# A diffusion-backbone layer: the mixer's output stage in written order, the output projection by pairs of tiles, and the sums of the down weights sooner

## The chip, the cores and the metric

The kernel runs on one core of one Trainium2 chip. A core has TensorE (PE, matrix products into PSUM), VectorE (DVE), ScalarE (ACT), GpSimd (POOL) and SyncE (SP); SP's queue issues all DMA transfers of this kernel, and 16 DMA engines carry them out. The metric is the device time of one execution in microseconds (us). The time before is 2552.67 us, median of three runs (2550.52 to 2553.85).

## The reference, cut to what matters

One layer with a short gated convolution and a bidirectional mLSTM side by side, then a gated feed-forward part with a convolution in it. 128 context tokens and 2048 latent tokens pass through the same weights, 1024 channels, four mLSTM heads of 128.

```
h   = rmsnorm(x) * (1 + scale1) + shift1
z   = h @ w_in                       # sc_b, sc_c, sc_x, q, k, v, o, gates
y_sc = sc_b * conv3(sc_c * sc_x)
h_m  = rmsnorm_heads(mlstm_bidir(q, k, v, gates)) * mh_norm * sigmoid(o)
x   = x + gate1 * (concat(y_sc, h_m) @ w_out)
h2  = rmsnorm(x) * (1 + scale2) + shift2
a, g = split(conv3(h2 @ w_up))
x   = x + gate2 * ((silu(g) * a) @ w_down)
y   = rmsnorm(x) * final_norm
```

The mLSTM is computed in chunks of 128 tokens. For a chunk the output is (scores * weights) @ v plus (query * weight) @ state for both directions, divided by a denominator, and the two directions are added.

## The kernel before, in words

All activations lie channels first. The 2176 tokens are six blocks of 384 (the last 256): BA is blocks 0 to 2, BB blocks 3 to 5. A block has two or three chunks; there are 17. Every large product is done with operands split into a rounded high part and a remainder (wh and wl for weights, hH and hL for activations): `gemm` (L201) is 8 k of three products, 24 matmuls, and `load_w` (L108) brings one weight tile of 128 output channels from DRAM (wst, two buffers), rounds it on ACT (L112) and makes the remainder on POOL in two halves (L115); wh and wl have four buffers.

The first part (to L596) computes modulation and norms, then, for BB, `vg` (v and gates), `heads` for k and q (each writes one head of a block to DRAM), `shortconv`, and the sigmoid of o. Generators of side work run between the gemms: `first_stats`, `mod_dve` (32 modulation columns on VectorE), and, in a generator of its own, `down_sums` (L554), which reads w_down, forms the sums that the last stage's seven-product scheme needs and writes them to DRAM (wsD). In the kernel before, the down sums run beside the gate projections of BB and the v projection of BA (L590 to L596). The block's activations for BA are made between them (`make_h`), in the buffers (three) that BB leaves. All this lies in a pool "start", whose memory the gate phase uses next.

`gate_phase` (L646) turns the gates into per-token weights, with k heads of BA as filler. Then `weave` (L890) runs `Sums` over the chunks from last to first (states of the backward direction, written to sD), and then `Mix` over 34 units, a unit being one chunk and two of the four heads. In each turn `weave` calls the stages of neighbouring units and then takes one or two steps of a filler: q heads, o heads, `shortconv` of BA, then 32 of the 48 steps of `out_proj`. In a Mix unit, `rows` loads R (512 KB, rows broadcast to all partitions, four buffers), `pre` adds the mask on POOL (L823) and takes the exponential on ACT (L827), `first` multiplies keys with queries (L834), weighs the queries (L837, into qs) and the scores (L838), `second` computes the output (L849, L851), the forward state (L855), denominators (L859 to L861) and the normed heads (L866 to L873), `third` transposes (L879) and gates with o (L881), `last` stores to yD (L886).

`out_proj` (L431) runs over three pairs of blocks. For each pair it goes through the eight output tiles m, and for each m through both blocks: a gemm with y, the gated residual (L462), the store to xD (L464), and the sum of squares (L466 to L470). `load_y` loads and splits the y of a block once all its chunks are done (L426 to L429). After Mix, `sums` (L226) builds operands of the up projection from xD and the norms, with the rest of `out_proj` between, and the up stage follows (L1045 to L1060), then the down stage (L1199).

What sets the order: the code is traced in the order of the program, and a planner then orders the instructions of each engine by the order of the program, by when its cost model has their operands and buffers ready, and by free buffers. Each engine, and SP's queue, then takes its instructions strictly in that order. An edge without a semaphore between two instructions of one engine fixes their order; `pin` (L106) does that for the loads and the additions in `down_sums`.

Of the kernel before, what the change touches and what calls it, by code (L numbers as in the profile page):

```python
# [18 lines left out]
P = 128  # L19
D = 1024  # L20
KT = 8
# [36 lines left out]
def hymba_kernel(ctx: ExitStack, tc: tile.TileContext, I, O):  # L58
# [49 lines left out]
    def load_w(src, n=1024):  # L108
        st = wp.tile([P, WN], F32, name="wst", bufs=2)
        Q.dma_start(st[:, :n], src)  # L110
        wh = wp.tile([P, WN], F32R, name="wh")
        S.activation(wh[:, :n], st[:, :n], AF.Copy)  # L112
        wl = wp.tile([P, WN], F32R, name="wl")
        for a in (0, n // 2):
            G.tensor_sub(wl[:, a:a + n // 2], st[:, a:a + n // 2], wh[:, a:a + n // 2].bitcast(F32))  # L115
        return wh, wl
# [200 lines left out]
    with ExitStack() as ph1:  # L317
# [66 lines left out]
        def shortconv(blocks, hs, then=None):  # L384
            for m in range(4):
                wc, wx, wb = (load_w(I["w_in"][o + m]) for o in (4, 8, 0))
                for b in blocks:
# [3 lines left out]
                    S.activation(cr[:, :n], acc[:, :n], AF.Copy)  # L391
                    yield
# [4 lines left out]
                    for s0, s1, v in spans(t0, t0 + n):  # L397
# [6 lines left out]
                                               yy[:, :, :w - 1], op0=ALU.mult, op1=ALU.add)  # L404
                    yield
# [3 lines left out]
                    if then and m == 3 and b != 1:  # L409
                        then(b // 2)  # L410
# [8 lines left out]
        def load_y(b):  # L419

            assert done >= set(chunks(b))
            t0, n = BL[b]
            yH, yL = early[b] = h_pair()
            for kh in range(2):
                yt = xp.tile([P, 4, 384], F32, name="xt")
                Q.dma_start(yt[:, :, :n], yD[4 * kh:4 * kh + 4, :, t0:t0 + n].rearrange("k p t -> p k t"))  # L426
                for k in range(4):
                    S.activation(yH[:, 4 * kh + k, :n], yt[:, k, :n], AF.Copy)
                    V.tensor_sub(yL[:, 4 * kh + k, :n], yt[:, k, :n], yH[:, 4 * kh + k, :n].bitcast(F32))  # L429

        def out_proj(grps, defer):  # L431


            def load_r(grp, m):
                xs_ = []
                for b in grp:
# [3 lines left out]
                    xs_.append(xr)  # L440
                return xs_

            seq = [(g, m) for g in range(len(grps)) for m in range(KT)]
            ws = [load_w(I["w_out"][m]) for _, m in seq[:2]]
            nx = load_r(grps[0], 0)
            for i, (g, m) in enumerate(seq):
                grp = grps[g]
                if m == 0:
                    sss = [ssp.tile([P, 384], F32, name="ss") for _ in grp]
                w, xs_ = ws.pop(0), nx  # L450
                if i + 1 < len(seq):
                    nx = load_r(grps[seq[i + 1][0]], seq[i + 1][1])
                if i + 2 < len(seq):
                    ws.append(load_w(I["w_out"][seq[i + 2][1]]))
                if g + 1 < len(grps) and m == (4, 7)[min(g, 1)]:
                    load_y(grps[g + 1][0])
                for b, ss, xr in zip(grp, sss, xs_):
                    t0, n = BL[b]
                    acc = gemm(w, early[b], n)
                    for a, e, v in spans(t0, t0 + n):  # L460
                        a, e = a - t0, e - t0
                        V.scalar_tensor_tensor(xr[:, a:e], acc[:, a:e], modT[:, 16 + m, v:v + 1], xr[:, a:e],  # L462
                                               op0=ALU.mult, op1=ALU.add)
                    Q.dma_start(xD[m][:, t0:t0 + n], xr[:, :n])  # L464
                    if m == 0:
                        S.activation(ss[:, :n], xr[:, :n], AF.Square)  # L466
                    else:
                        sq = sqp.tile([P, 384], F32, name="sq")
                        S.activation(sq[:, :n], xr[:, :n], AF.Square)
                        V.tensor_add(ss[:, :n], ss[:, :n], sq[:, :n])  # L470
                    if m == KT - 1 and b == grp[1 - g] and g + 1 < len(grps):
                        load_y(grps[g + 1][1])
                    yield
                if m == KT - 1:
                    if g == len(grps) - 1:
                        defer.append(lambda: stats(grp, sss))
                    else:
                        stats(grp, sss)
# [3 lines left out]
        with tc.tile_pool(name="start", bufs=1, side="right") as stp:  # L482
# [104 lines left out]
            side = chain(first_stats(), mod_dve())  # L587
# [5 lines left out]
            run(shortconv(BB, hs), side)  # L593
            run(side)
            go = heads(BB, hs, 20, oD, AF.Sigmoid, 1.0, by_block=True)
            dsums = down_sums()  # L596
            for b in BA:
                run(islice(go, 4), dsums)
                hs[b] = make_h(b, I["x"], 0)
            run(vg(BA, hs, load_vg(0) + load_vg(1)), dsums)  # L600
            run(dsums)
# [148 lines left out]
        class Sums:  # L750
# [42 lines left out]
            def nothing(self):  # L793
                pass

            rows = pre = third = last = nothing

        class Mix:
# [21 lines left out]
            def pre(self):  # L820
                c, hp, R = self.c, self.hp, self.R
                W = R[:, :, 0]
                G.tensor_add(W, W, bc(maskN[:, None], [P, 2, 2, P]))  # L823
                acol = colsel(self.cols, AC, max(c, 0), hp)
# [4 lines left out]
            def first(self):  # L829
                c, R = self.c, self.R  # L830
                W = R[:, :, 0]
                psS = pm.tile([P, 512], F32, name="S")
                for h in range(2):
                    PE.matmul(psS[:, h * P:(h + 1) * P], self.k2[:, h], self.q2[:, h], start=True, stop=True)  # L834
                if c >= 0:
                    self.qs = mb.tile([P, 2, 2, P], F32, name="qs", bufs=2)
                    V.tensor_tensor(self.qs, R[:, :, 1], bc(self.q2[:, :, None, :], [P, 2, 2, P]), op=ALU.mult)  # L837
                V.tensor_tensor(W, bc(psS[:, :256].rearrange("p (h t) -> p h t", h=2)[:, :, None, :],  # L838
                                      [P, 2, 2, P]), W, op=ALU.mult)

            def second(self):
                c, hp, sf = self.c, self.hp, sfs[self.hp]
                self.o2 = load2(mb, "o2", oD, c + 1, hp, 5)
                y = pm.tile([P, 2, 512], F32, name="y", bufs=2)
                for h in range(2):
                    for d in range(2):
                        o = y[:, h, d * 129:(d + 1) * 129]
                        if c >= 0:
                            PE.matmul(o, self.qs[:, h, d], sf[:, h] if d == 0 else self.sb[:, h, 1],  # L849
                                      start=True, stop=False)  # L850
                        PE.matmul(o, self.R[:, h, 0, d], self.v2[:, h], start=c < 0, stop=True)  # L851
                if 0 <= c < NL - 1:
# [4 lines left out]
                yv = y[:, :, :258].rearrange("p h (d n) -> p h d n", d=2)  # L857
                den = mb.tile([P, 2, 2], F32, name="den", bufs=2)
                V.tensor_tensor(den, yv[:, :, :, 128], colsel(self.cols, EM, max(c, 0), hp), op=ALU.max)  # L859
                V.scalar_tensor_tensor(den, yv[:, :, :, 128], -1.0, den, op0=ALU.mult, op1=ALU.max)  # L860
                V.reciprocal(den, den)  # L861
                hv = self.hv = mb.tile([P, 2, P], F32, name="hv", bufs=3)
                ss = mb.tile([P, 2], F32, name="hss", bufs=2)
                sj = mb.tile([P, P], F32, name="sj", bufs=2)
                for h in range(2):
                    S.activation(hv[:, h], yv[:, h, 0, :P], AF.Copy, scale=den[:, h, 0:1])  # L866
                    V.scalar_tensor_tensor(hv[:, h], yv[:, h, 1, :P], den[:, h, 1:2], hv[:, h],
                                           op0=ALU.mult, op1=ALU.add)
                    S.activation(sj, hv[:, h], AF.Square, accum_out=ss[:, h:h + 1])
                V.tensor_scalar(ss, ss, 1.0 / P, EPS, op0=ALU.mult, op1=ALU.add)  # L870
                G.tensor_tensor(ss, ss, mhalf[:, :2], op=ALU.pow)
                for h in range(2):
                    S.activation(hv[:, h], hv[:, h], AF.Copy, scale=ss[:, h:h + 1])  # L873

            def third(self):
                c, hp, o2 = self.c, self.hp, self.o2
                psT = pst.tile([P, 512], F32, name="st")
                for h in range(2):
                    PE.transpose(psT[:, h * P:(h + 1) * P], self.hv[:, h], ident)  # L879
                for h in range(2):  # L880
                    V.scalar_tensor_tensor(o2[:, h], psT[:, h * P:(h + 1) * P], mhn[:, 2 * hp + h:2 * hp + h + 1], o2[:, h],  # L881
# [8 lines left out]
        def weave(units, fill, extra):  # L890

            n = len(units)
            for i in range(-2, n + 4):
                for k, stage in ((-1, "second"), (0, "first"), (-3, "third"), (-4, "last"), (1, "pre"), (1, "load"), (2, "rows")):
                    if 0 <= i + k < n:
                        getattr(units[i + k], stage)()
                if not -1 <= i < n + 3:
                    continue
                next(fill, None)
                if extra and i % extra == 0:  # L900
                    next(fill, None)


# [404 lines left out]
```

## Time and profile before

| | |
|---|---|
| median of three runs | 2552.67 us |
| the profiled execution | 2555.34 us, span 2553.5 us |
| TensorE busy | 2470.7 us, 97% |
| VectorE, ScalarE, GpSimd busy | 1649.2, 1112.7, 566.4 us |
| mean granted TensorE clock | 0.985 |
| DMA | 444.60 MB, mean 174 GB/s |

In the page's groups, an instruction's time includes its way through the pipeline, so a group's sum can be more than its engine's busy time; busy times by stretches are those of the engine, with overlaps counted once. "PEclk" is the TensorE clock granted, as a share of the full one. Waits are given as the waiting instruction, what released it, and total, number and longest in us. A DMA share is the mean busy share of the 16 DMA engines.

### The profile page before, as it was taken

How to read it: one execution, taken by the hardware profiler on the slowest of the kernel's cores; microseconds unless marked ns; L12 is line 12 of the kernel's file. 1: busy time of each engine (PE TensorE's matmuls, PEld its weight loads, DVE VectorE, ACT ScalarE, POOL GpSimd, SP SyncE). 2: the span in 40 equal slices, each digit the busy share in tenths (PEclk: the TensorE clock that was granted, in tenths of full speed). 3: DMA queues.
4: the chain of work that ended last, by engine and by line, in shares of the span. 5: the costliest groups of instructions: out<-in, count | busy, mean ns of one | idle time of the engine just before them, and what ended most of it. 6: DMA issues, size and time to landing. Idle time of an engine off the chain costs nothing.

```text
span 2553.5 us, 42533 instructions
## 1 busy us (share of the span) xinstructions
PE 2470.7 (97%) x16127; PEld 2366.4 (93%) x16127; DVE 1649.2 (65%) x2741; ACT 1112.7 (44%) x2035; POOL 566.4 (22%) x470
## 2 busy tenths in 40 slices
PE   8999998999999889899999999899999999999998
PEld 8999997999999889899999999788888899999998
DVE  3993255222356666678678666877776796687586
ACT  4522142222245554455455444555554554444342
POOL 2442142211233443422112111122122100000000
PEclk9999998999999999999999999999999999999999
DMA  7771188356567887775125222522222277767674
GB/s 280 252 270 69 66 278 284 117 168 178 180 191 241 253 261 226 251 270 173 67 81 181 83 83 82 171 92 99 83 91 93 72 227 227 242 214 225 187 218 135
DMA packets 281423, 444.60 MB, mean 174 GB/s; under 512 B 23282, under 2 KB 206722, under 8 KB 279554
## 3 DMA queue, kind: packets, MB, share of 16 engines
q1 hardware_dynamic: 281218, 441.88, 53.0%
q8 instruction: 127, 2.08, 0.3%
q14 instruction: 78, 0.64, 0.1%
HBM read 335.31 MB, written 106.48 MB: 173 GB/s over the span
## 4 chain that ended last, share of the span: by engine, by line
PE 77%; DMA 8%; DVE 7%; issue 3%; ACT 3%; POOL 2%; SPq 1%; DVEq 0%; ACTq 0%; POOLq 0%
PE acc L206 8%; PE acc L208 8%; PE acc L207 8%; PE pa L1045 7%; PE pa L1047 7%; PE pa L1046 6%; PE d L1200 5%; PE d L1201 5%; PE d L1199 5%; PE pb L1045 3%; PE pb L1046 3%; PE pb L1047 3%; PE pc L1045 2%; PE pc L1046 2%; PE pc L1047 2%
## 5 line engine op out<-in xcount | busy, mean ns | idle before, releaser
L206 PE MATMUL acc<-hH,wh 128*128 128x384 f32 (+1 forms) x1536 | 515.4, 336 | 8.2 <-DVE row L462 5.5
L208 PE MATMUL acc<-hH,wl 128*128 128x384 f32 (+1 forms) x1536 | 508.0, 331 | 0.5 <-POOL wl L115 0.5
L207 PE MATMUL acc<-hL,wh 128*128 128x384 f32 (+1 forms) x1536 | 507.8, 331 | 0.0
L1199 PE MATMUL d<-bh,wh 128*128 128x272 f32 x1232 | 355.7, 289 | 0.7 <-ACT raw L1057 0.7
L1201 PE MATMUL d<-bh,wl 128*128 128x272 f32 x1232 | 356.1, 289 | 0.0
L1200 PE MATMUL d<-bl,wh 128*128 128x272 f32 x1232 | 355.4, 289 | 0.0
L1045 PE MATMUL pa<-tH,wh 128*128 128x288 f32 (+1 forms) x1056 | 347.7, 329 | 3.7 <-DVE raw L1059 2.0
L1047 PE MATMUL pa<-tH,wl 128*128 128x288 f32 (+1 forms) x1056 | 346.9, 329 | 1.0 <-DVE wl L296 1.0
L1046 PE MATMUL pa<-tL,wh 128*128 128x288 f32 (+1 forms) x1056 | 346.9, 329 | 0.0
L296 POOL TENSOR_TENSOR wl<-st,wh 128x512 fp32r<-128x512 f32 x132 | 184.2, 1396 | 696.2 <-ACT wh L295 668.4
L115 POOL TENSOR_TENSOR wl<-wst,wh 128x512 fp32r<-128x512 f32 (+1 forms) x160 | 235.2, 1491 | 441.8 <-ACT wh L112 417.5
L206 PEld LDWEIGHTS acc<-hH,wh 128*128 128x128 f32 x1536 | 292.9, 191 | 10.2 <-DVE row L462 5.1
L208 PEld LDWEIGHTS acc<-hH,wl 128*128 128x128 f32 x1536 | 292.6, 190 | 1.2 <-POOL wl L115 1.0
L207 PEld LDWEIGHTS acc<-hL,wh 128*128 128x128 f32 x1536 | 293.1, 191 | 0.3 <-issue 0.2
L988 DVE SCALAR_TENSOR_TENSOR tt<-raw,fw,tt 128x127 f32<-128x127 f32 (+4 forms) x264 | 246.1, 953 | 2.7 <-ACT tt L994 1.5
L1199 PEld LDWEIGHTS d<-bh,wh 128*128 128x128 f32 x1232 | 231.9, 188 | 1.3 <-ACT raw L1057 1.1
L1200 PEld LDWEIGHTS d<-bl,wh 128*128 128x128 f32 x1232 | 231.9, 188 | 0.2
L1201 PEld LDWEIGHTS d<-bh,wl 128*128 128x128 f32 x1232 | 231.8, 188 | 0.0
L1045 PEld LDWEIGHTS pa<-tH,wh 128*128 128x128 f32 x1056 | 198.4, 188 | 20.2 <-ACT c L1052 2.2
L1047 PEld LDWEIGHTS pa<-tH,wl 128*128 128x128 f32 x1056 | 199.1, 189 | 17.0 <-DVE wl L296 1.4
L1046 PEld LDWEIGHTS pa<-tL,wh 128*128 128x128 f32 x1056 | 198.7, 188 | 15.7
L295 ACT ACTIVATE wh<-s 128x512 fp32r<-128x512 f32 x176 | 110.9, 630 | 177.7 <-PE pc L1046 92.0
(239 smaller groups left out, 4848.6 us busy)
## 6 DMA issues: line engine op xcount, KB each, us to landing
st<-in_w_up SPq DMA_DIRECT2D x88, 512.0 KB, 4.3
us<-uD SPq DMA_DIRECT2D x48, 544.0 KB, 5.0
wst<-in_w_in SPq DMA_DIRECT2D x48, 512.0 KB, 4.0
uD<-tt SPq DMA_DIRECT2D x44, 544.0 KB, 2.7
R<-nD SPq DMA_DIRECT2D x34, 512.0 KB, 4.2
wm<-in_w_modr SPq DMA_DIRECT2D x32, 512.0 KB, 5.2
wst<-in_w_out SPq DMA_DIRECT2D x24, 512.0 KB, 4.7
st<-wsD SPq DMA_DIRECT2D x32, 384.0 KB, 3.3
```

Of the source, the lines that this page charges most:

```text
L115: G.tensor_sub(wl[:, a:a + n // 2], st[:, a:a + n // 2], wh[:, a:a + n // 2].bitcast(F32))
L206: PE.matmul(acc[:, :n], w_h, hH[:, k, :n], start=(k == 0), stop=False)
L207: PE.matmul(acc[:, :n], w_h, hL[:, k, :n], start=False, stop=False)
L208: PE.matmul(acc[:, :n], w_l, hH[:, k, :n], start=False, stop=(k == KT - 1))
L296: (G if on_pool else V).tensor_sub(wl, a, wh.bitcast(F32))
L988: V.scalar_tensor_tensor(o, i, w, o, op0=ALU.mult, op1=ALU.add)
L1045: PE.matmul(acc, wh[:, w], rh, start=(kk == 0 and i in (0, 1, 5)), stop=False, skip_group_check=True)
L1046: PE.matmul(acc, wh[:, w], rl, start=False, stop=False, skip_group_check=True)
L1047: PE.matmul(acc, wl[:, w], rh, start=False, stop=(kk == 3), skip_group_check=True)
L1199: PE.matmul(acc, wh[:, c], uh, start=(kk == 0), stop=False)
L1200: PE.matmul(acc, wh[:, c], ul, start=False, stop=False)
L1201: PE.matmul(acc, wl[:, c], uh, start=False, stop=(kk == KH - 1))
```

## The change

Three things change; the arithmetic stays.

In Mix the five methods become fifteen small stages, and `weave` gets two lists: stages called before the filler and stages called after it. The edges added by `in_order` fix, for every instruction from the first to the last of the Mix weave, the order of the program on its engine, SP's queue and the filler included. The product of queries and weights is made in place in R, so the tile qs goes.

`out_proj` goes by pairs of tiles: m and m+1 for one block, then for the other. A weight is loaded four steps ahead and split two steps later; the store and the squares of a step come at the start of the next one; the statistics of a pair of blocks come after the next pair's first gemm; y is loaded and split in steps. `shortconv` loads and splits the next tile's weights at given points, and ends with the first two weights of `out_proj`.

`down_sums` is chained behind `mod_dve` in the side work of BB, and what is left of it is run before the start pool closes; the v projection of BA comes after that pool.

```diff
+    def in_order(first):
+        behind = {}
+        for i in nc.cur_bb.bb.instructions[first:]:
+            if i.engine in behind:
+                tc.add_manual_dep(i, behind[i.engine].name, mybir.DependencyInfo(
+                    mybir.DependencyClass.NoSync, mybir.DependencyReason.DATA), reason="in_order")
+            behind[i.engine] = i
...
-        def shortconv(blocks, hs, then=None):
+        def shortconv(blocks, hs, then=None, more=(), ws=None):
+            todo = chain((I["w_in"][o + m] for m in range(4) for o in (4, 8, 0)), more)
+            ws = [] if ws is None else ws
+            ws += [load_w(next(todo)) for _ in range(3)]
...
+        def next_y(grp, ready):
+            for b, may in zip(grp, ready):
+                while not done >= set(chunks(b)):
+                    yield
+                yts = get_y(b)
+                yield
+                for kh in range(2):
+                    while not may():
+                        yield
+                    split_y(b, yts, kh)
+                    yield
+
+        def out_proj(grps, defer, ws):
+            steps = [(g, m, b) for g, grp in enumerate(grps) for mp in range(0, KT, 2) for b in grp for m in (mp, mp + 1)]
...
+            for k, (g, m, b) in enumerate(steps):
...
+                for x in behind:
+                    close(*x)
+                load_r(k + 2)
+                if k + 4 < len(steps):
+                    if k % 4 < 2:
+                        got.append(get_w(I["w_out"][steps[k - k % 4 + 4 + k % 4][1]]))
                     else:
+                        ws.append(split_w(got.pop(0)))
+                w, xr = ws[m % 2], rows.pop(0)
+                if 0 < k < 3:
+                    load_y(grps[0][1], k)
+                elif k % 16 >= 5:
+                    next(ny, None)
+                acc = gemm(w, early[b], n)
+                if k % 4 == 3:
+                    del ws[:2]
+                for x in held:
+                    stats(*x)
...
-            side = chain(first_stats(), mod_dve())
+            side = chain(first_stats(), mod_dve(), down_sums())
...
             run(shortconv(BB, hs), side)
+            go = heads(BB, hs, 20, oD, AF.Sigmoid, 1.0, by_block=True)
+            for b in BA:
+                run(islice(go, 4), side)
+                hs[b] = make_h(b, I["x"], 0)
             run(side)
-            go = heads(BB, hs, 20, oD, AF.Sigmoid, 1.0, by_block=True)
-            dsums = down_sums()
-            for b in BA:
-                run(islice(go, 4), dsums)
-                hs[b] = make_h(b, I["x"], 0)
-            run(vg(BA, hs, load_vg(0) + load_vg(1)), dsums)
-            run(dsums)
...
-                    self.qs = mb.tile([P, 2, 2, P], F32, name="qs", bufs=2)
-                    V.tensor_tensor(self.qs, R[:, :, 1], bc(self.q2[:, :, None, :], [P, 2, 2, P]), op=ALU.mult)
+                    Z = self.R[:, :, 1]
+                    V.tensor_tensor(Z, Z, bc(self.q2[:, :, None, :], [P, 2, 2, P]), op=ALU.mult)
...
+        def weave(units, fill, extra, ahead, behind):
+            n, x = len(units), max(k for k, _ in ahead)
+            for i in range(-x, n + 4):
+                for k, stage in ahead:
                     if 0 <= i + k < n:
                         getattr(units[i + k], stage)()
+                if -1 <= i < n + 3:
+                    next(fill, None)
+                    if extra and i % extra == 0:
                         next(fill, None)
+                for k, stage in behind:
+                    if 0 <= i + k < n:
+                        getattr(units[i + k], stage)()
+        run(vg(BA, hs, load_vg(0) + load_vg(1)))
...
+        first = len(nc.cur_bb.bb.instructions)
+        weave([Mix(c, hp) for c in range(-1, NL) for hp in range(2)], fill, 3,
+              ((2, "rows"), (1, "load"), (-2, "gate"), (-4, "last"), (1, "exps"),
+               (-1, "out"), (0, "scores"), (-3, "turn"), (0, "queries"), (-2, "norm"), (-1, "denom"), (0, "weigh"),
+               (-3, "third"), (-1, "heads"), (-2, "scale")), ((2, "mask"),))
+        in_order(first)
```

215 lines of the change are left out of this document (127 added, 88 removed).

## The prediction

> **What bounds the kernel now.** I read the page first, its busy shares.
>
> ```profile
> span 2553.5 us, 42533 instructions
> PE 2470.7 (97%) x16127; PEld 2366.4 (93%) x16127; DVE 1649.2 (65%) x2741; ACT 1112.7 (44%) x2035; POOL 566.4 (22%) x470
> ```
>
> TensorE does nothing for 2553.5 - 2470.7 = 82.8 us, and that, with the time in which its clock is granted lower, is all that a change of order can win. So the second view is the busy time of every engine by stretches, cut at the stages that the change touches.
>
> ```profile
> core 0: us, PE busy (x) PEld busy (x) DVE busy (x) ACT busy (x) POOL busy (x), PEclk, DMA share, GB/s
> 370.00:400.00 30.00, 21.79 (x160) 21.12 (x159) 26.84 (x35) 13.61 (x27) 18.22 (x16) 0.89 0.84 283
> 400.00:430.00 30.00, 30.00 (x251) 30.00 (x250) 12.14 (x22) 3.48 (x10) 0.71 (x7) 1.00 0.91 312
> 430.00:450.00 20.00, 14.17 (x72) 12.86 (x71) 8.71 (x30) 8.27 (x12) 6.48 (x8) 0.74 0.75 255
> 706.00:806.00 100.00, 100.00 (x663) 100.00 (x662) 54.85 (x159) 50.72 (x156) 38.50 (x34) 1.00 0.68 216
> 806.00:1002.00 196.00, 176.14 (x1125) 173.61 (x1124) 130.76 (x341) 104.47 (x314) 81.43 (x70) 0.96 0.81 253
> 1050.00:1150.00 100.00, 88.65 (x582) 87.17 (x583) 70.70 (x113) 48.35 (x82) 28.50 (x23) 0.93 0.82 273
> ```
>
> Three stretches lose time that this change can reach. 806 to 1002 is the mixer's output stage once the output projection is its filler: 196 - 176.14 = 19.9 us idle, and (1 - 0.96) x 196 = 7.8 us of clock. 370 to 400 is where the BA half's projections start beside the sums of the down weights: 8.2 idle, 0.11 x 30 = 3.3 of clock. 430 to 450 is the start of the gate phase: 5.8 idle, 0.26 x 20 = 5.2 of clock. Together 27.7 + 11.5 + 11.0 = 50.2 us. The stretch 706 to 806, the same stage with the short convolution as filler, loses nothing, and that has to stay so. The stretch after it, 1050 to 1150, loses 11.4 idle to the sums for the up projection, which the change leaves alone.
>
> Third, who waits. Of TensorE between 690 and 1010, then of the DMA queue of SP between 700 and 1010:
>
> ```profile
> PE y L851 <- DVE R L838: 14.9, 7, 4.4
> ...
> SPq L886 <- DVE hv L867: 35.2, 15, 4.3
> SPq L742 <- DMA yD<-o: 20.7, 13, 4.5
> SPq L439 <- DMA xD<-row: 16.8, 11, 4.1
> ```
>
> The output products (L851) wait for the weighted scores (L838) seven times. Behind that, SP stands at stores of one unit (L886) while loads of the next wait behind it.
>
> **The mixer stage.** Pace first, from the first, thirteenth and last weighing on VectorE:
>
> ```profile
> 706.13 0.68 DVE L838 TENSOR_TENSOR R<-S,R 128x512 f32<-128x512 f32 x1
> ...
> 805.71 0.68 DVE L838 TENSOR_TENSOR R<-S,R 128x512 f32<-128x512 f32 x1
> ...
> 1002.03 0.69 DVE L838 TENSOR_TENSOR R<-S,R 128x512 f32<-128x512 f32 x1
> ```
>
> Twelve units took 99.6 us, 8.30 each; the next 21 took 196.3, 9.35 each. At the first pace the 21 cost 174.3, so 22.0 us less. The new order takes no instruction away but the copy into qs, which becomes a product in place (same shape, same time). What it does is put every engine's queue in the order written. I follow one unit by these rows of the stage:
>
> ```profile
> R<-nD SPq DMA_DIRECT2D x30, 512.0 KB, 4.2
> L823 POOL TENSOR_TENSOR R<-R,maskN 128x512 f32<-128x512 f32 x30 | 40.9, 1364 | 77.0 <-DMA R<-nD 56.6 <-PE y L851 7.1 <-PE acc L208 6.9
> L827 ACT ACTIVATE R<-R,cols 128x128 f32<-128x128 f32 x120 | 41.7, 391 | 40.1 <-POOL R L823 40.1
> L838 DVE TENSOR_TENSOR R<-S,R 128x512 f32<-128x512 f32 x32 | 21.7, 679 | 0.0
> L115 POOL TENSOR_TENSOR wl<-wst,wh 128x512 fp32r<-128x512 f32 x36 | 48.3, 1362 | 53.3 <-ACT wh L112 46.2 <-PE y L849 4.5 <-PE st L879 2.6
> L429 DVE TENSOR_TENSOR hL<-xt,hH 128x384 fp32r<-128x384 f32 x38 | 23.1, 642 | 17.1 <-ACT hH L428 17.1
> L462 DVE SCALAR_TENSOR_TENSOR row<-acc,modT,row 128x384 f32<-128x384 f32 x15 | 9.2, 611 | 1.5 <-PE acc L208 1.5
> ```
>
> R for unit i+2 is asked for in turn i; its buffer (four) is freed by the products of unit i-2 at the start of turn i-1. The mask runs on POOL at the end of turn i, the exponentials on ACT at the start of turn i+1, the weighing on VectorE in turn i+2, and the products in turn i+3. The path 4.2 + 1.36 + 4 x 0.39 + 0.68 = 7.8 us is thus spread over more than two turns of 8.3 us, so each step has a turn of slack. The new waits: a DVE queue that waits for a gemm's end (L462) holds the next turn's query product and denominators, but the products of that next turn already have their weighing. SP now waits at the store of xD for L462 with the next turn's loads behind it; these are wanted a turn later. POOL's mask stands behind two to four halves of L115, 1.36 each; the exponentials have until the next turn. So the 14.9 us of L851 go, and with them the clock they cost. What is late next is DMA: the stage keeps its bytes, so 0.81 x 196 = 158.8 us of full DMA must fit the shorter stage. At the 0.91 that the row of 400 to 430 held it takes 174.5, a gain of 21.5; at the 0.82 of 1050 to 1150 it takes 193.7, a gain of 2.3. The other end is the whole 27.7. I take 21, near the first, because the written order hands SP a whole turn's loads at once, as in the row with 0.91, and because the pace says 22.
>
> **Pairs of tiles.** The gemms, loads and stores are as many as before; only the order changes (m, m+1 of one block, then of the other), and weights are fetched four steps ahead and split two steps ahead, within the same four and two buffers. Cost 0, covered by the gemms between. Two places are worse. Rows: one product of a gemm and the same product one k later, a weight's copy, a y's copy.
>
> ```profile
> 705.56 0.34 PE L208 MATMUL acc<-hH,wl 128*128 128x384 f32 x1
> ...
> 706.09 0.34 PE L208 MATMUL acc<-hH,wl 128*128 128x384 f32 x1
> ...
> L112 ACT ACTIVATE wh<-wst 128x1024 fp32r<-128x1024 f32 x18 | 18.9, 1049 | 9.0 <-DMA wst<-in_w_out 9.0
> L428 ACT ACTIVATE hH<-xt 128x384 fp32r<-128x384 f32 x39 | 17.8, 512 | 7.1 <-DMA xt<-yD 7.1
> ```
>
> A k of three products takes 0.53 us, a gemm of eight k 4.2. The second block's y is split in the step that first uses it: a gemm reaches its fifth k after 4 x 0.53 = 2.1 us, while the step before's L462 (0.61), a square (taken as L428's 0.51), a weight's copy (1.05) and the fifth k's copy and remainder (0.51 + 0.64) come to 3.3, and later k follow at 0.64: 1.5 us, between 0 and 3. And the statistics of a group stand behind the next group's first gemm, 4.2 us, and the sums of the next stage wait for them: 2, between 0 and 4.2. Together +3.5.
>
> **Sums of the down weights.** In the side work they stand behind 38 steps (six of statistics, 32 modulation columns), and 48 side steps are taken by the end of BB's short convolution (6 + 6 + 36); so ten of their 25 steps run there, twelve between the gate projections as now, and the last three at once, before the BA half's v projection. Rows of SP, POOL, DVE and ACT around both idle stretches:
>
> ```profile
> 330.95 1.99 SPq L566 DMA_DIRECT2D xs<-in_w_down  x4
> 380.40 0.72 SPq L110 DMA_DIRECT2D wst<-in_w_vg  x1
> 430.19 5.38 DMA wsD<-xs
> 434.10 0.28 PE L354 MATMUL acc<-wh,hL 128*128 128x264 f32 x1
> 435.37 0.42 SPq L110 DMA_DIRECT2D wst<-in_w_in  x1
> L576 DVE TENSOR_TENSOR xs<-xs x6: 892/1252/2002, 373.4 to 423.6; 128x704 f32<-128x704 f32 x6
> 389.23 1.53 POOL L115 TENSOR_TENSOR wl<-wst,wh 128x528 fp32r<-128x528 f32 x1 [0.39 <-ACT wh L112]
> PE S L665 <- DVE fc L658: 4.9, 1, 4.9
> 275.00:370.00 95.00, 95.00 (x625) 95.00 (x624) 33.72 (x58) 30.32 (x59) 26.15 (x25) 1.00 0.49 170
> wst<-in_w_in SPq DMA_DIRECT2D x48, 512.0 KB, 4.0
> ```
>
> Today the fourth v weight is asked for at 380.40, behind stores of the sums, and its remainder begins at 389.23; VectorE meanwhile works on the sums' rows (L576 to L580) from 373.4. Without the middle sums in the queue and on VectorE it comes sooner, but the two staging buffers still keep it waiting for the second weight. Of 11.5 I take 6, half, between 0 and 11.5. At the gate phase the first key weight is asked for at 435.37, after the last product of the v projection (434.10); the sums' stores, whose last lands at 435.6 and frees the gate phase's memory, are gone by then. Two key gemms stand ahead of the transposes in the program, so if their weights are there the 4.9 us wait is filled; if the planner puts the transposes first, as now, it stays. Of 11.0 I take 6, between 1 and 11. Their new place, 275 to 314, has DMA at 0.49 and VectorE at 33.7 of 95: cost 0, covered by 95 us of gemms whose weights come a tile ahead; without that cover one weight's landing, 4 us.
>
> **Sum.** -21 + 3.5 - 6 - 6 = -29.5 us. The profiled execution took 2555.34 us for its span of 2553.5; the median of the runs is 2552.67. So 2525.8 as profiled, 2523 as a median.
>
> **Rivals.** First, DMA is the next bound: at the 0.82 share the mixer gives 2.3 us, the rest stays, -10.8: 2542. For it: the stage is at 0.81 already; against: 30 us at 0.91 in this trace. If the planner's order had been as good as the written one and R merely lands late, that is, the change does not do what it says, the number is the same. Chance 0.20 for the two.
>
> Second, everything goes: 50.2 less 1.5, 2504. For it: 253 x 196 / 168.3 = 295 GB/s would be needed, and 400 to 430 held 312; against: the small transfers of the mixer. Chance 0.13. The Trainium skill, page "DMA: Bandwidth & Descriptors", section "Bandwidth", measures 341 GB/s for transfers of 1 MB and gives 435 as the ceiling; by these 295 binds nowhere and this rival would be the forecast. The stage's own share of 0.81 at 253 GB/s, which makes 312 at a share of 1, says that its transfers do not reach that.
>
> Third, slower: the fixed order on SP. One late VectorE step now holds SP at the xD or yD store, R lands a turn later than I reckon, and mask, exponentials and weighing follow in queues that may no longer pass each other. If each of 34 units waits the 2.1 us that L851's waits have on average (14.9 / 7), that is 71.4, less the 14.9 of now, with the clock not won back: +56.5 + 3.5 - 12 = +48, so 2601. It decides from 29.5 / 34 = 0.87 us for each unit. Against it: the turn of slack above, and VectorE at 131 of 196. Chance 0.09.
>
> **How the numbers follow.** Forecast 0.56, with its own range 2508 to 2538; first rival 0.20 (2538 to 2549), second 0.13 (2500 to 2508), third 0.09, nothing at all 0.02. The measurement tells about 0.2%, 5.1 us. Faster by more: 0.56 + 0.13 + two thirds of the first rival = 0.82; within: 0.07 + 0.02 = 0.09; slower 0.09. The range 2504 to 2548 leaves out the third, the upper end of the first and half the second.
>
> **What would show it.** Right: no wait of L851 on L838; TensorE full from the first unit to the last at 8.3 to 8.5 us a unit, DMA near 0.91; the sums' loads before 314 and no store of wsD after 380; gemms in 434 to 440. Wrong: waits in the first twelve units; DMA share over 0.9 with the pace still over 9; the fourth v weight as late as now; the stage of the up sums longer by what the mixer saved.

## The result: 0.8% slower, all of it in the mixer stage

The changed kernel takes 2573.62 us (median of four runs, 2569.19 to 2575.84), the kernel before 2553.26 beside it (2550.52 to 2558.14). The ratio is 1.0082, 95% interval 1.0064 to 1.01: slower, where 2523 was forecast. The profiled execution took 2571.62 us for a span of 2569.8. The page of the changed kernel, its span and busy times:

```profile
span 2569.8 us, 42565 instructions
...
PE 2470.9 (96%) x16127; PEld 2365.3 (92%) x16127; DVE 1663.5 (65%) x2741; ACT 1109.0 (43%) x2035; POOL 575.0 (22%) x470
```

TensorE is busy for the same time as before, to 0.2 us, over a span that is 16.3 us longer. The weighings of the changed kernel on VectorE, first, thirteenth and last, say where (start, duration, instruction):

```profile
704.53 0.69 DVE L932 TENSOR_TENSOR R<-S,R 128x512 f32<-128x512 f32 x1
...
815.36 0.68 DVE L932 TENSOR_TENSOR R<-S,R 128x512 f32<-128x512 f32 x1
...
1018.84 0.68 DVE L932 TENSOR_TENSOR R<-S,R 128x512 f32<-128x512 f32 x1
```

The first comes 1.6 us sooner than before. From the first to the last it takes 314.3 us instead of 295.9, which is +18.4: twelve units at 9.24 us instead of 8.30, then 21 at 9.69 instead of 9.35. After the last weighing nothing changes by more than 0.5 us (the up stage starts 117.4 us later in both, and then has 1433.6 us to the end instead of 1434.1). -1.6 + 18.4 - 0.5 = 16.3, the difference of the spans. In what follows "the stretch" is the time from the first to the last weighing. One row for the stretch, before and then after (busy us of the engines, granted clock, DMA share, GB/s):

```profile
706.10:1002.00 295.90, 276.04 (x1785) 273.51 (x1785) 185.51 (x499) 155.19 (x469) 119.93 (x104) 0.97 0.77 240
```

```profile
704.50:1018.80 314.30, 284.20 (x1781) 278.85 (x1780) 195.15 (x496) 149.96 (x468) 116.75 (x101) 0.94 0.73 234
```

TensorE idles 30.1 us instead of 19.9, so +10.2, and the same products take 284.2 us instead of 276.0, so +8.2, at a clock of 0.94 instead of 0.97. DMA moves less per second than before; it is no bound here. The stretches that the prediction cut, in the changed kernel:

```profile
core 0: us, PE busy (x) PEld busy (x) DVE busy (x) ACT busy (x) POOL busy (x), PEclk, DMA share, GB/s
370.00:400.00 30.00, 13.03 (x86) 12.21 (x86) 19.86 (x29) 11.43 (x21) 15.56 (x11) 0.72 0.77 274
400.00:430.00 30.00, 28.65 (x234) 28.23 (x234) 1.78 (x14) 4.26 (x10) 3.69 (x13) 1.00 0.44 128
430.00:450.00 20.00, 20.00 (x154) 20.00 (x153) 4.19 (x11) 9.08 (x13) 10.27 (x10) 1.00 0.38 120
706.00:806.00 100.00, 94.28 (x593) 93.74 (x592) 51.42 (x144) 42.84 (x134) 36.43 (x32) 0.95 0.59 190
806.00:1002.00 196.00, 171.62 (x1062) 166.81 (x1061) 129.70 (x316) 98.99 (x307) 72.10 (x64) 0.93 0.79 255
...
275.00:370.00 95.00, 95.00 (x626) 95.00 (x625) 49.26 (x78) 31.46 (x63) 26.70 (x25) 1.00 0.77 269
```

706 to 806 was full and is not; 806 to 1002 has not filled. 430 to 450 is full, but it now holds the end of the v projection, which ends 10.4 us later than before; the start of the gate phase, now 445 to 465, is full as well (20.00 of 20 at a clock of 1.00). 370 to 400 lost about what the gate phase won. Who waits in the mixer stage of the changed kernel, TensorE from 690 to 1010 first, then SP's queue from 700 to 1010 (total us, times, longest):

```profile
PE S L923 <- DMA q<-qD: 7.6, 3, 3.8
PE st L144 <- DVE rc L147: 7.5, 1, 7.5
PE y L944 <- DVE R L932: 6.6, 6, 3.1
PE acc L221 <- ACT hH L482: 6.6, 2, 6.3
```

```profile
SPq L449 <- DVE yr L448: 77.6, 8, 12.5
SPq L524 <- DVE row L563: 45.3, 12, 8.6
```

The wait of the output products for the weighing (14.9 us before, L851 then) is 6.6 now, so that part of the change works in part. Three waits are new or larger: for q (7.6), for the statistics (7.5; L144 behind L147), for y's split (6.6; L221 behind L482). The four rows are 28.3 of the 30.1 us that TensorE idles. SP now stands 77.6 us at eight stores of the short convolution's output (L449). One of these in the changed kernel's order of time on SP:

```profile
768.59 0.41 SPq L997 DMA_DIRECT2D yD<-o  x1
781.56 0.33 SPq L449 DMA_DIRECT2D yD<-yr  x1
781.99 0.37 SPq L906 DMA_DIRECT2D R<-nD  x1
782.42 0.44 SPq L835 DMA_DIRECT2D k<-kD  x1
782.91 0.46 SPq L840 DMA_DIRECT2D v<-vD  x1
783.42 0.43 SPq L835 DMA_DIRECT2D q<-qD  x1
```

For 12.6 us, one and a half turns, nothing is asked for; then R, k, v and q of the next units go out at once, and the q of a unit is wanted in the turn after the one that asks for it.

### The profile page after: what moved, and what is told of

It reads as the page before. It is cut to its first block, busy times and chain, and to the rows that moved or that the text cites. A ratio compares the mean times of both kernels' runs of the same rounds, so it can differ in the third digit from the quotient of the medians.

```text
span 2569.8 us, 42565 instructions
## 1 busy us (share of the span) xinstructions
PE 2470.9 (96%) x16127; PEld 2365.3 (92%) x16127; DVE 1663.5 (65%) x2741; ACT 1109.0 (43%) x2035; POOL 575.0 (22%) x470
## 4 chain that ended last, share of the span: by engine, by line
PE 80%; DVE 7%; DMA 6%; issue 2%; POOL 2%; ACT 2%; SPq 0%; DVEq 0%; POOLq 0%; ACTq 0%
PE acc L221 8%; PE acc L223 8%; PE acc L222 8%; PE pa L1167 6%; PE pa L1169 6%; PE pa L1168 6%; PE d L1322 5%; PE d L1323 5%; PE d L1321 5%; PE pb L1167 3%; PE pb L1169 3%; PE pb L1168 3%; PE pc L1167 2%; PE pc L1168 2%; PE pc L1169 2%
## 5 line engine op out<-in xcount | busy, mean ns | idle before, releaser
L221 PE MATMUL acc<-hH,wh 128*128 128x384 f32 (+1 forms) x1536 | 514.9, 335 | 12.5 <-ACT hH L482 6.6
L221 PEld LDWEIGHTS acc<-hH,wh 128*128 128x128 f32 x1536 | 292.7, 191 | 14.6 <-ACT hH L482 7.2
```

Source lines behind the costliest of these rows:

```text
L221: PE.matmul(acc[:, :n], w_h, hH[:, k, :n], start=(k == 0), stop=False)
```

## Experiments

### Which engine's order costs it, and what the sums bring alone

a1 leaves SP to the planner, a2 holds SP alone, a3 holds nothing (the call of `in_order` is out); a4 is the kernel before with the sums of the down weights moved and nothing else.

```diff
         for i in nc.cur_bb.bb.instructions[first:]:
+            if i.engine == mybir.EngineType.SP:      # a1; a2 has != in its place
+                continue
```

> The changed kernel, with SP's queue left out of the fixed order; PE, DVE, ACT and POOL keep it. Measure: from the first to the last weighing of the mixer (295.9 us before, 314.3 in the changed kernel) and the time (2573.6 changed, 2553.3 before). If the loss comes from SP's queue (stores that wait for the filler hold the next turn's loads): 285 to 298 us and 2543 to 2557 in time, and no TensorE wait on a load of q. If it comes from the order on the four engines: over 308 us and over 2567. If from the pairs of tiles: as the changed kernel.

> The reverse: only SP's queue keeps the written order, the four engines are ordered by the planner. SP's queue as the cause: 308 us or more for the mixer and 2567 or more. The engines' order as the cause: under 300 us and under 2560. Pairs of tiles: about 314.

> The changed kernel without the fixed order on any engine; stages, pairs of tiles and sooner sums stay. If the fixed order is the cause: 300 us or less for the mixer, 2545 to 2560. If the pairs of tiles or the way in which y is split in steps are the cause: 308 or more and 2567 or more.

> The kernel before with the sums of the down weights sooner, and nothing else of the change. By the prediction 12 us faster than before: 2541. By the trace of the changed kernel, whose first mixer weighing comes 1.6 us sooner and whose later stages do not gain from it: 2550 to 2554, with a TensorE wait of 10 to 18 us before the v projection of BA and none at the gate phase.

| run | time, us | ratio to before, 95% interval | first weighing at | stretch |
|---|---|---|---|---|
| a1, SP free | 2552.47 | 1.0017 [1.0004, 1.0029] | 705.9 | 297.5 |
| a2, SP alone | 2553.8 | 1.0015 [1.0004, 1.0027] | 705.6 | 295.7 |
| a3, no order | 2550.7 | 1.0011 [0.9999, 1.0022] | 703.7 | 297.5 |
| a4, sums alone | 2549.13 | 0.9998 [0.9985, 1.001] | 705.9 | 296.1 |

These times, and those further down, come from different batches, in which the kernel before had medians from 2545.2 to 2553.3, so compare the ratios and not the times. Each stretch is read from one execution. That of the kernel before took 2555.34, more than its medians beside the experiments (2545.2 to 2548.5), so a stretch can show less of a loss than the ratio.

SP's order is needed for the loss (a1) and is not enough for it (a2). With SP free it stands only 6.5 us at the store of the short convolution, and TensorE has no wait for q. With SP alone held it stands there 75.9 us, about as long as in the changed kernel, and TensorE still waits 6.6 us for q; but the waits for y's split and the statistics are 4.0 and 1.8 us instead of 7.9 (copies and remainders together) and 7.5. Held together they cost 18 in the stretch. Pairs of tiles and stages cut finer bring nothing of their own in the planner's order (a3), nor do the sums (a4).

### Late loads: b1 to b4 and c1

Within the strict order, b1 asks for R three turns ahead and for the other loads two (one buffer more for R); b2 puts the mask ahead of the turn's exponentials instead of behind the filler; b3 asks for the first v weights ahead of the sums that are left; b4 does all three. c1 leaves the loads and issues nine of the twelve stores of the short convolution one step of the filler later, behind the next turn's loads.

```diff
-              ((2, "rows"), (1, "load"), ...            ((2, "mask"),))
+              ((3, "rows"), (2, "load"), ...            # b1, with R in five buffers
+              (-4, "last"), (1, "mask"), (1, "exps"), ...      ())      # b2
...
+            wv = load_vg(0) + load_vg(1)                # b3
             run(side)
-        run(vg(BA, hs, load_vg(0) + load_vg(1)))
+        run(vg(BA, hs, wv))
...
+                    while pend:                         # c1, ahead of the step's first gemm
+                        Q.dma_start(*pend.pop())
...
-                    Q.dma_start(yD[m][:, t0:t0 + n], yr[:, :n])
+                    if then and m < 3:
+                        pend.append((yD[m][:, t0:t0 + n], yr[:, :n]))
+                    else:
+                        Q.dma_start(yD[m][:, t0:t0 + n], yr[:, :n])
```

> The changed kernel, all queues in the written order, with R and the unit's other loads asked for one turn sooner (R three turns ahead in five buffers instead of two in four, k, q, v and state two turns ahead instead of one). If the fixed order loses because SP, held by a store, brings loads a few us after they are wanted: the waits on q go, the mixer (first to last weighing, 314.3 us) falls to 285 to 300, time 2545 to 2558. If the loss is in the order of the engines' own work (the mask behind the splits): over 308 and over 2567.

> The changed kernel with the mask before the filler and one turn later (unit i+1 at the head of turn i, ahead of its exponentials), so that on POOL it no longer stands behind the splits of the filler's weights. If the late mask holds ACT and with it the heads and the weighing: 300 us or less for the mixer and under 2560. If SP's loads are the cause: 310 or more and over 2567; worse than the changed kernel if the slack of R was needed.

> The changed kernel with the four weights of the v projection of BA asked for before the rest of the sums instead of after it. If the wait of 14.9 us before the v projection comes from the weights' place behind the sums' transfers: that wait falls under 6 us, the mixer begins 7 to 12 us sooner, and the time falls by as much, to 2561 to 2567. If it is the traffic itself: no more than 3 us.

> All three together. If each takes its own wait away: mixer 275 to 292 us, the v projection 7 to 12 us sooner, time 2520 to 2545, better than the kernel before (2548.5 to 2553). If DMA bounds the mixer: DMA share over 0.9 from the thirteenth unit on, with the pace still over 9 us a unit, and 2545 to 2560.

> The strict order stays on all engines; only the short convolution's store of its output (nine of the twelve in the Mixer stage) is issued one filling step later, so behind the next turn's loads on SP instead of ahead of them. Theory (SP stands at this store, 77.6 us at eight stores in the changed kernel, and the loads behind it land after they are wanted): the waits for yr at this store fall from 77.6 to under 30 us, the waits for q of PE and DVE (7.6 and 9.9) to under 3, the stretch from the first to the last weighing from 314.3 to 298-304, the time to 2557-2564, as with the loads a turn sooner. Rival (what holds SP is any order of stores and loads in one queue, the next store in it takes the stand over): SP waits as long at the xD or Mixer store, stretch 310-315, time 2570-2576.

| run | time, us | ratio to before, 95% interval | first weighing at | stretch |
|---|---|---|---|---|
| changed kernel | 2573.62 | 1.0082 [1.0064, 1.01] | 704.5 | 314.3 |
| b1, loads sooner | 2560.12 | 1.0037 [1.002, 1.0054] | 703.7 | 299.6 |
| b2, mask first | 2568.38 | 1.0072 [1.005, 1.0094] | 705.2 | 311.3 |
| b3, v weights first | 2564.5 | 1.0056 [1.0039, 1.0073] | 699.9 | 310.8 |
| b4, all three | 2554.25 | 1.0029 [1.0011, 1.0046] | 699.4 | 300.5 |
| c1, y store later | 2564.64 | 1.007 [1.0047, 1.0092] | 707.3 | 303.8 |

TensorE's waits in the mixer stage of b1:

```profile
PE st L144 <- DVE rc L147: 7.9, 1, 7.9
PE acc L221 <- ACT hH L482: 6.6, 2, 6.1
PE y L944 <- DVE R L932: 5.9, 5, 2.7
```

TensorE's wait for q is gone, and with it 14.7 of the 18.4 us of the stretch, though SP still stands 63.2 us at the same store. So what is lost is the slack of the loads behind the store, not SP's time. (b1 moves R as well, but TensorE's waits for the weighing only go from 6.6 to 5.9.) By ratio less comes back, 0.37% of loss instead of 0.82, and b1's time lies 2 us above the range expected. c1 comes at it from the other side and gives 10.5 us of the stretch back, at the weak end of what was expected; by ratio it can't be told from the changed kernel. The waits for q go only from 7.6 to 5.1. SP's queue in the mixer stage of c1 shows why:

```profile
SPq L529 <- DVE row L568: 44.7, 13, 8.2
SPq L454 <- DVE yr L450: 28.6, 3, 12.4
SPq L421 <- DVE yr L450: 26.8, 5, 8.5
SPq L911 <- PE y L949: 15.8, 6, 6.2
```

SP's waits for yr were to fall under 30 us and fall to 55.4: the stores that were moved (L421) cost 26.8, the three that were not (L454) still 28.6, and the load of R, now ahead of them, stands 15.8 for its buffer. b3 belongs to the sums: TensorE's wait for the v weights falls from 14.9 to 8.9 us, and the first weighing comes 4.6 sooner, less than expected (under 6, and 7 to 12 sooner). Its edit lies ahead of the stretch, and the stretch still reads 3.5 us less; the 3.0 of b2 are no more than that, so the mask's place is not shown to be worth anything. b4 misses its expectation of 275 to 292: with 300.5 its stretch is that of b1 alone, since the waits for the statistics (7.9) and for y's split (6.6) stay.

### The pairs of tiles: c2

Strict order and the loads' places stay. The first two rows of x are asked for six steps of the filler sooner; y's split stands behind the residual of the steps before the one that needs it; the last y of the next pair is split behind the statistics.

```diff
             rows, got, behind, held, sss, past = rows0, [], [], [], {}, set()   # rows0: loaded with the first y
-            for k in range(2):
-                load_r(k)
...
-                if 0 < k < 3:
-                    load_y(grps[0][1], k)
-                elif k % 16 >= 5:
+                if k % 16 >= 5:
                     next(ny, None)
...
                 past.add((b, m))
+                if k < 2:
+                    load_y(grps[0][1], k + 1)
+                run(tail)
                 behind = [(b, m, xr)]
                 if k % 16 == 15:
-                    run(ny)
+                    tail = ny
```

> The strict order and the loads' places stay. Moved: the first two rows of x for the output projection are loaded six filling steps sooner, the second tile's y is split behind the residual of the steps before instead of ahead of the gemm that uses it, and the last y of the next pair is split behind the statistics of the pair before instead of ahead of them. Theory (the pairs of tiles cost three waits of PE that the strict order doesn't let anything fill, 6.6 for the y split, 7.5 for the statistics, and a part of 8.3 for the first rows, and the clock granted falls to 0.53-0.74 in the ten us after each): stretch from first to last weighing from 314.3 to 296-303, time 2555-2564. Rival (what PE waits for there is only what it would wait for a step later, since the loads are late anyway): stretch 310-315, time 2568-2575.

2561.8 us, ratio 1.0056 [1.0038, 1.0075], stretch 298.6: 15.7 us less than the changed kernel, as the theory had it; by ratio 0.26 of the 0.82% come back, and the two intervals overlap. The places at fault, in the changed kernel's order of time on VectorE, each with the idle time before it and what ended it, then SP's:

```profile
853.53 0.74 DVE L563 SCALAR_TENSOR_TENSOR row<-acc,modT,row 128x128 f32<-128x128 f32 x2 [8.26 <-DMA row<-in_x]
...
969.06 4.00 DVE L483 TENSOR_TENSOR hL<-xt,hH 128x384 fp32r<-128x384 f32 x8 [3.22 <-ACT hH L482]
972.98 0.55 DVE L530 TENSOR_TENSOR ss<-ss,sq 128x384 f32<-128x384 f32 x1
973.44 0.15 DVE L147 TENSOR_SCALAR rc<-st 128x3 f32<-128x3 f32 x1
```

```profile
846.76 1.83 SPq L518 DMA_DIRECT2D row<-in_x  x3
...
961.47 2.56 SPq L471 DMA_DIRECT2D xt<-yD  x2
```

The first rows are asked for at 846.76, in the step that adds them to its product; VectorE stands 8.26 us, with the next turn's queries and denominators behind it. The y asked for at 961.47 is split at once, all eight tiles of it in one step, and the statistics' 0.15 us on VectorE (L147) stands behind that for 7.5 us of TensorE's time. In c2 that wait is 1.1 us and the one for y's split gone; the waits for q stay (9.4 us). So late loads and the pairs' places are two causes.

### Everything moved, in both orders: c4, d1, and the sums in the kernel before: c3

c4 is b4, c1 and c2 together. d1 is c4 without the call of `in_order`. c3 is a4 with the v weights first, in the planner's order.

> The changed kernel in strict order with everything that the runs so far put right: loads and mask sooner, v weights first, short convolution's store a step later, and the three waits of the pairs of tiles moved. Theory (the strict order itself is sound, and the loss lay in the places of a few steps): the stretch from first to last weighing at 284-293 (PE's work there is 277 us at full clock), first weighing at 699-700, time 2535-2545, 0.2 to 0.6% under the kernel before. Rival (a fixed order on SP and on the engines together always loses what the free order fills): stretch 296-302, time 2548-2556.

> All steps as in c4_all_moved, but no engine and no queue is held to the program's order: the scheduler places them, as in the kernel before. Theory A (the fixed order is worth something of its own once its steps stand right): stretch from first to last weighing 293-299, as in the run without the order, against 287.7; time 2543-2552. Theory B (what the moved steps bring, they bring in either order): stretch 285-291, time 2535-2542.

> The kernel before with the sums of the down weights sooner (as in a4) and the v weights of the first tiles loaded ahead of the sums that are left. Theory (sooner sums bring 2 to 6 us once the v projection doesn't wait for its weights behind their stores): v projection's end at 437-440 instead of 444.5, first weighing at 699-701 instead of 706, time 0.1 to 0.4% under the kernel before. Rival (the time gained ahead of the Mixer stage is lost again in what follows): first weighing at 699-701, time within 0.1% of the kernel before.

| run | time, us | ratio to before, 95% interval | first weighing at | stretch |
|---|---|---|---|---|
| c4, all moved, strict | 2538.33 | 0.997 [0.9958, 0.9983] | 699.2 | 287.7 |
| d1, all moved, planner's order | 2547.53 | 1.0003 [0.999, 1.0016] | 701.5 | 298.8 |
| c3, sums and v weights, planner's order | 2542.9 | 0.9991 [0.9977, 1.0005] | 697.1 | 292.3 |

The row of the stretch in c4:

```profile
699.20:986.90 287.70, 275.73 (x1781) 271.89 (x1780) 195.03 (x497) 149.04 (x468) 117.20 (x101) 0.98 0.77 247
```

TensorE idles 12.0 us in the stretch, against 19.9 before and 30.1 in the changed kernel, at a clock of 0.98. b1 gave 14.7 us back and c2 15.7, together more than was lost; c4, which has both, is 26.6 shorter than the changed kernel. The idle times add up (7.2 less in b1, 10.4 in c2, 18.1 in c4), the time of the same products does not (7.5, 5.3 and 8.5 less). c4 is 0.3% faster than the kernel before, the only one of the runs that is. The same steps in the planner's order (d1) bring nothing that can be told from no change. So a written order does bring something here, but only with each step in its place. c3 has the sooner start (697.1) and a time that this measurement cannot tell from no change.

### The other half beside SP: d2 and d3

The changed kernel with the order held on SP and VectorE alone (d2), and on SP and TensorE alone (d3); for d3:

```diff
         for i in nc.cur_bb.bb.instructions[first:]:
+            if i.engine not in (mybir.EngineType.SP, mybir.EngineType.PE):
+                continue
```

> The changed kernel with the program's order held on SP and VectorE alone, TensorE, ScalarE and GpSimd free. Order on SP alone cost 0 us in the stretch (295.7), on the four engines alone 2 (297.5), on both 18 (314.3). Theory (VectorE is the other half: its late results hold SP's stores, and where it stands for a load, nothing of its other work is pulled forward): stretch 308-316, time 2565-2575. Rival (TensorE's order is the other half): stretch 295-301, time 2548-2557.

> The changed kernel with the program's order held on SP and TensorE alone, VectorE, ScalarE and GpSimd free. Theory (VectorE is the other half of the loss): stretch 295-301, time 2548-2557. Rival (TensorE is: a product that waits for a late load can't be passed by another): stretch 308-316, time 2565-2575.

d2: 2553.77 us, 1.0027 [1.0012, 1.0041], stretch 291.3. d3: 2565.47 us, 1.0079 [1.0058, 1.0101], stretch 305.3. My theory of VectorE falls. TensorE's waits for q in the mixer stage, in d2 and then in d3:

```profile
PE S L925 <- DMA q<-qD: 3.1, 5, 1.6
```

```profile
PE S L925 <- DMA q<-qD: 20.4, 10, 6.2
```

With TensorE's order free, the scores wait 3.1 us for q; with it held, 20.4, and the gemm behind them may not go first. That is not the whole of it, since the changed kernel holds TensorE too and waits 7.6. By its stretch d3 lies between the two expectations, 9.4 of the 18.4 us; by its ratio it has the whole loss (1.0079 against 1.0082). So TensorE is the other half by time, and whether the orders of the remaining engines add to the loss stays open: the one stretch says so, the ratio does not.

## Why the prediction was wrong, by its own steps

**What bounds.** The 50.2 us of idle time and clock were there to be won. c4 wins some of it; the changed kernel won the 11.0 of the gate phase, lost about as much ahead of it, and lost 18.4 in the mixer.

**The mixer stage, -21: measured +18.4 for the stretch.** The step that failed is "each step has a turn of slack". It followed R, which is asked for two turns ahead, and not q, which is asked for one turn ahead and wanted by TensorE and VectorE at the start of the next. And it took a wait of SP at the store as less than a turn; it lasts up to 12.5 us where a turn has 8.3. The store at which it lasts so long is that of the short convolution (77.6 us), which the prediction's list of new waits leaves out; it names the store of xD, which has 45.3 with a longest of 8.6. "These are wanted a turn later" is what b1 makes true: with a turn more the waits for q are gone and 14.7 us come back. The sentence on SP handing out "a whole turn's loads at once" came true as bursts. Windows of the changed kernel around the stand shown above:

```profile
770.00:780.00 10.00, 7.04 (x48) 6.66 (x46) 7.84 (x14) 5.12 (x16) 6.13 (x5) 0.97 0.21 69
780.00:790.00 10.00, 9.91 (x47) 9.91 (x48) 4.95 (x18) 4.86 (x20) 2.19 (x3) 0.69 0.70 234
860.00:870.00 10.00, 2.97 (x13) 2.16 (x12) 7.33 (x21) 7.03 (x21) 2.60 (x3) 0.74 1.02 336
870.00:880.00 10.00, 9.48 (x39) 8.47 (x40) 6.83 (x15) 1.90 (x6) 3.44 (x3) 0.58 0.23 71
```

A DMA share of 1.02 stands beside one of 0.23: an even 0.91 was the forecast's condition, and bursts with holes do not give it. What held in part is that the 14.9 us of the weighing's wait go: 6.6 are left, and 5.3 even in c4.

**Pairs of tiles, +3.5: measured 15.7 (c2).** Size and one place failed. y's split was put at 1.5, at most 3, by the durations of copies; TensorE waited 6.6, because in the strict order ACT came to the second half only behind the rest of the turn, which itself waits for the denominators. ScalarE of the changed kernel, in order of time (the half that was waited for is the last row):

```profile
864.02 0.62 ACT L965 ACTIVATE hv<-y,den 128x128 f32<-128x128 f32 x2 [2.01 <-DVE den L957]
...
867.22 1.04 ACT L127 ACTIVATE wh<-wst 128x1024 fp32r<-128x1024 f32 x1
868.17 1.75 ACT L482 ACTIVATE hH<-xt 128x384 fp32r<-128x384 f32 x4
```

The statistics were put at 2, at most 4.2, for the gemm ahead of them; the 7.5 came from the y split ahead of them on VectorE. The first rows of x, in the step that uses them, were not seen at all: 8.26 us of VectorE. Of the 15.7, 10.4 are idle time; the other 5.3 are the same products in less time, at a clock of 0.97 instead of 0.94.

**Sums of the down weights, -6 and -6: measured -1.6 at the first weighing.** The gate phase's half was right and undersized: its start, 445 to 465 now, has TensorE at 20.00 where 430 to 450 had 14.17, and the clock at 1.00, so all of the 11.0 us. The new place costs nothing, as said (95.00 of 95 with VectorE at 49.26 and DMA at 0.77). The other half had the wrong sign. The step was "without the middle sums in the queue and on VectorE it comes sooner": the stores of the last sums stand in SP's queue ahead of the v weights, now all of them. TensorE's wait there in the changed kernel, and SP:

```profile
PE acc L367 <- ACT wh L127: 14.9, 1, 14.9
```

```profile
376.93 2.21 SPq L679 DMA_DIRECT2D wsD<-xs  x4
379.18 1.76 SPq L119 DMA_DIRECT2D wst<-in_w_vg  x2
388.27 5.43 SPq L679 DMA_DIRECT2D wsD<-xs  x4
394.55 0.33 SPq L119 DMA_DIRECT2D wst<-in_w_vg  x1
```

The first two weights go out at 379.18, the third at 394.55, behind four more stores. In the kernel before the fourth had gone out at 380.40. The v projection ends 10.4 us later (445.0 instead of 434.6), and the gate phase gives that back. The end of stores at 380, named as a sign, is not there.

**The rivals.** DMA as the next bound falls: share 0.73 in the stretch. The second rival, which wins everything, needed 295 GB/s; 860 to 870 moved 336 at a share of 1.02, so the rate was there in bursts, and what stopped the gain was not DMA. The third rival named the right place and most of the mechanism (SP at the yD and xD stores behind a late VectorE, with the queues unable to pass each other), though with R as the late load instead of q, and was given 0.09; its price, 48 us, was too high, since not each of 34 units waits: TensorE waits three times for q and six for the weighing. It should have had more, because SP's row of before (L886) showed it standing 35.2 us at stores in a queue that the planner could still arrange. Of the signs, the first ("waits in the first twelve units") decided it: 5.7 us idle in 706 to 806.

## What to carry to other kernels

When a queue's order is fixed, count the slack of every load behind each store in it, from the end of the work that the store waits for, and not of the largest load alone; then give the loads the turn that the store can take. The same goes for each engine: an instruction that waits for something asked for in its own step holds all of the next turn. A written order over engines and DMA queue together leaves no one to make up for a misplaced step: look for such steps one by one, after which it can beat a planner, here by 0.3%.

## What the hardware showed that I had not expected

A long wait of TensorE is paid twice. The 3.05 us for which it waits up to 780.09 in the changed kernel are followed by ten us at a clock of 0.69, in which 47 products run where the 100 us of this stage in the kernel before had 663, so 66 in ten; the products of a gemm start 0.32 us apart up to 786.2, and 0.17 to 0.18 after that. After the 7 idle us of 860 to 870 the next ten run at 0.58. The waits of 3.76 and 7.54 us are followed by the same 0.32. Near 2.7 us it goes either way: after 2.67 in the changed kernel (up to 728.38) the products start 0.32 apart, after 2.70 in b1 (up to 774.53) the clock stays at 1.00. In the whole stretch 10.2 us more of idle time came with 8.2 more for the same products. The Trainium skill, page "TensorE: Matmul & The Clock Gate", section "Part 1: The HAM clock gate", says that the clock halves after an idle window of about 3.4 us and comes back after as long a busy one. These rows agree in kind; here 2.67 us of idle time were once enough, and the old pace came back 3.3 us (728.38) to 6.1 us (780.09) after the wait.
